# A decoder trunk on one core: VectorE takes the first convolution behind block 2's masked shares, and the third weight tile's low half behind the first normed row

## The chip, the cores and the metric

The kernel runs on one core of a Trainium2 chip. The time is what the device takes for one execution, in microseconds (us). An execution is also profiled; the profile has its own time and its own span (first instruction to last), a little shorter than that time. In the profile PE is TensorE (matmuls), PEld its weight loads, DVE is VectorE, ACT ScalarE, POOL GpSimd and SP SyncE, which issues the loads of the weights. PE, DVE and ACT each work through one list of instructions in a fixed order; an instruction whose operands are not there holds up all that stand behind it on its engine.

## The reference

The input `x` is 512 tokens of 1024 numbers. Two layers follow each other, each of three sub-layers, each with an RMS norm ahead of it that is scaled and shifted by terms made from `c`:

```python
for l in range(DEPTH):                                   # DEPTH = 2
    hn = rms_norm(h, g_ffn1[l]) * (1.0 + sc1) + sh1
    h = h + 0.5 * (1.0 + gt1) * swiglu(hn, w_ffn1_in[l], w_ffn1_out[l])     # 1024 -> 2816 -> 1024
    hn = rms_norm(h, g_mix[l]) * (1.0 + sc2) + sh2
    proj = hn @ w_mix_in[l]
    p_att, p_rwkv, p_conv = jnp.split(proj, ...)
    y_att = sliding_window_sink_attention(p_att, ...)    # window 128, blocks of 128 tokens, 2 groups of heads
    y_rwkv = rwkv7_time_mix(p_rwkv, ...)                 # a recurrence over the tokens, 4 heads of 64
    y_conv = short_conv_mix(p_conv, conv_w[l])           # three taps over time
    h = h + (1.0 + gt2) * (jnp.concatenate([y_att, y_rwkv, y_conv], axis=-1) @ w_mix_out[l])
    hn = rms_norm(h, g_ffn2[l]) * (1.0 + sc3) + sh3
    h = h + 0.5 * (1.0 + gt3) * swiglu(hn, w_ffn2_in[l], w_ffn2_out[l])
```

The convolution that the change moves is this one; `u` and the three taps are its first four operations on VectorE:

```python
b_gate, c_gate, h = jnp.split(p, [CONV_WIDTH, 2 * CONV_WIDTH], axis=-1)
u = c_gate * h
y[t] = w[2] * u[t] + w[1] * u[t - 1] + w[0] * u[t - 2]    # the convolution, written out
return b_gate * y
```

## The kernel before, in words

**Layout.** The activations stand transposed: `h` and the normed `hn` are 8 row blocks of 128 channels by 512 tokens. A matmul in full precision is three matmuls on halves of the numbers (`mm3`, lines 129 to 131): high weights by high activations, high weights by low activations, low weights by high activations. So every weight tile (128 x 1024, loaded as `wraw`) is split before use: ACT copies the high half (`wH`, line 141), DVE subtracts to get the low half (`wL`, line 143). The activations are split too: normed row `i` is `hn_t` (DVE, line 290), `hnH` (ACT, line 291), `hnL` (DVE, line 292).

**The order.** The program is written as generators and a planner in `mix` that steps them by a running clock with hand-set costs; the result is a fixed list per engine. `tc.issue_after(x)` puts what is issued inside it right behind `x` in its engine's list, `queue_behind(name)` does that with the latest instruction noted under a name, and `tc.add_manual_dep(later, earlier, ORDER)` only pins an order.

**The seam** (function `ffn`, lines 696 to 728). The last two row blocks of a feed-forward part's output, 6 and 7, are computed for the first 256 tokens, then for the second 256 (`HALVES`). While PE works on the second half, the norm of the first half is made: `stats` sums the squares over the channels (`ps_ss`, line 273), `spread` brings the result to all partitions (`ps_rstd`, line 283), `apply` makes the eight normed rows. Also in that time the next sub-layer's first three weight tiles are split by `next_weights(3)`. The next sub-layer's projector begins with those three tiles together: for each row `k` of the first half nine matmuls (three `wH` by `hnH`, then for each tile `wH` by `hnL` and `wL` by `hnH`), then the same for the second half; the fourth tile comes after. There are three such seams: from the first feed-forward part to `mix` in both layers, and from layer 1's second feed-forward part to layer 2's first.

**The convolution spot** (function `mix`, twice, once per layer). `products` (lines 827 to 975) draws 20 projected tiles from the projector and uses each; a tile lies in one of two PSUM banks of the tag `mm` until DVE or ACT has read it. For the first of the two convolutions (`q == 0`) it makes `conv_u` (line 927), its first scaling `conv_y` (line 929), two more taps (lines 930 and 931) and the gate (line 933). Between these, other generators put their work: `inverse` inverts triangular blocks for the recurrence in two levels, each `ps_x` (PE), `X` (DVE, line 1128), `ps_t` (PE), `T_` and `TT` (DVE, line 1141); the recurrence then reads `TT` in `ps_w`. `attention` goes through four blocks of 128 tokens; for each block and group the normalised shares `Sc` are transposed (`ps_pt`, PE) and masked by DVE into `pmc` (own block) and `pmp` (the block before), line 1353; `ps_av` multiplies them with `V`. The list `held` keeps the two later taps and block 2's masked shares behind the last `X` of the second level:

```python
for later in held if lev else ():
    tc.add_manual_dep(later.ins, new.ins.name, ORDER, reason="the inverse goes first")
```

Of the kernel before, what the change touches and what calls it, by code (L numbers as in the profile page):

```python
# [8 lines left out]
F32 = mybir.dt.float32  # L9
F32R = mybir.dt.float32r  # L10
I32 = mybir.dt.int32
AF = mybir.ActivationFunctionType
ALU = mybir.AluOpType
AXL = mybir.AxisListType
ORDER = mybir.DependencyInfo(mybir.DependencyClass.NoSync, mybir.DependencyReason.DATA)
SYNC = mybir.DependencyInfo(mybir.DependencyClass.Sync, mybir.DependencyReason.DATA)

P = 128
D = 1024
T = 512  # L20
L = 2
KD = D // P
# [48 lines left out]
def trunk_kernel(ctx, tc, ins, out, layers=L, phases=("ffn1", "mix", "ffn2")):  # L71
    nc = tc.nc
# [4 lines left out]
    wp = ctx.enter_context(tc.tile_pool(name="wp", bufs=3))  # L77
# [5 lines left out]
    tt, stt, ts = nc.vector.tensor_tensor, nc.vector.scalar_tensor_tensor, nc.vector.tensor_scalar  # L83
# [51 lines left out]
    def queue_behind(name):  # L135
        return tc.issue_after(latest[name].ins) if name in latest else nullcontext()
# [97 lines left out]
    def ada_until(pool, crep, l, i):  # L234
        while todo and todo[0] <= (l, i, KD - 1):
            ada_steps(pool, crep, 1)
# [115 lines left out]
    def ffn(l, w_in, w_pair, w_out, hn, im, ss, need, then, first, ready, coming):  # L352
# [6 lines left out]
        with tc.tile_pool(name="act", bufs=1) as ap_:  # L359
# [342 lines left out]
            def next_weights(n):  # L702
                for w in raws[len(nxt) : n]:
                    nxt.append(tuple(wp.tile([P, KD, P], F32R, name=x, tag=x, bufs=4) for x in ("wH", "wL")))
                    split(*nxt[-1], w, ("act", "dve"))

            ada_until(ap_, crep, *need)
            stats, spread, apply = then()
            sqs = []
            for sl in HALVES:  # L710
                for i in (6, 7):
                    pt = psmm(BANKS[1:3])[:, : T // 2]
                    for j in range(j0, j1):
                        mm3(pt, last[i, j0 + (j - j0) // n * n], (j - j0) % n, xs[j], sl, j == j0, j == j1 - 1)
                        if sl is HALVES[1]:
                            if (i, j) == (6, j0 + 5):
                                stats(HALVES[0], sqs)
                                next_weights(3)
                            elif (i, j) == (7, j0):
                                spread(HALVES[0])  # L720
                                apply(HALVES[0])
                    if i == 6:
                        residual(pt, i, cg, ss, sl)
                        if sl is HALVES[0]:
                            next_weights(1)
                    else:
                        sqs = [last_residual(pt, i, cg, ss, sl)]
# [6 lines left out]
    def mix(l, hn, ss, mp, then, ready):  # L734
# [35 lines left out]
        cm = small_.tile([P, KD], F32, name="cm", tag="cg")  # L770
        ts(cm, mod[l, 5], 1.0, None, ALU.add)

        done, held, turns = set(), [], []
        k_, r_, v_, yr = {}, {}, {}, {}
        got = {}

# [50 lines left out]
        def products():  # L827
# [93 lines left out]
            for q in range(2):  # L921
                pt = yield from tile_()
                cc = EA("conv_c")
                nc.scalar.copy(pt.like(cc), pt.view)
                pt = yield from tile_()
                u = EA("conv_u")
                tt(pt.like(u), pt.view, pt.like(cc), ALU.mult)
                cv = mp.tile([P, T], F32, name="conv_y", tag="cv", bufs=1) if q == 0 else EA("conv_y")
                ts(cv, u, cwp[:, 4 + q : 5 + q], None, ALU.mult)
                held.append(stt(cv[:, 1:], u[:, : T - 1], cwp[:, 2 + q : 3 + q], cv[:, 1:], ALU.mult, ALU.add))  # L930
                held.append(stt(cv[:, 2:], u[:, : T - 2], cwp[:, q : q + 1], cv[:, 2:], ALU.mult, ALU.add))
                pt = yield from tile_()
                tt(pt.like(cv), pt.view, pt.like(cv), ALU.mult)
                yc.append(cv)
# [361 lines left out]
        def attention():  # L1296
# [62 lines left out]
            for b in range(NB):  # L1359
                qs = slice(b * P, (b + 1) * P)  # L1360
                pm = []
                both = yield from scores(b)
                dens = [softmax(b, g, Sc) for g, Sc in enumerate(both)]
                for g, (Sc, (den, es)) in enumerate(zip(both, dens)):
                    yield 1.06 * (g == 0), 6.4 if g == 0 else 1.2
                    tt(den, den, es, ALU.add)
                    nc.vector.reciprocal(den, den)
                    share = tt(Sc, Sc, den.unsqueeze(2).to_broadcast([P, 4, P]), ALU.mult)
                    for later in turns if (b, g) == (2, 0) else ():
                        tc.add_manual_dep(later.ins, share.ins.name, ORDER, reason="shares go first")  # L1370
                    yield 0, 1.4
                    pm.append(turned(b, Sc))
                yield 0.4, 3.0
                po = psum([P, 4, P], "ps_av")
                for n in range(len(pm[0])):
                    for g in range(2):
                        t, src = pm[g][n]
                        m = pe(po[rows[g]].rearrange("p i q -> p (i q)"), V[:, src, rows[g]], t, start=n == 0, stop=n == len(pm[0]) - 1)
                        together(m, made[0])
                free[0] = nc.scalar.copy(qr[:, :, qs], po)  # L1380
                yield 1.9, 1.0
# [349 lines left out]
```

## Time and profile before

| | us |
|---|---|
| median of 3 runs | 1795.22 (1794.1 to 1796.64) |
| the profiled execution | 1792.58 |
| its span | 1790.8 |
| PE busy | 1766.0 |
| PEld busy (beside PE) | 1613.3 |
| DVE busy | 1384.6 |
| ACT busy | 856.5 |
| POOL busy | 148.3 |

The mean granted clock of PE in the profiled execution is 0.999 of full speed. PE is the engine that is nearly always busy, so the table's other rows matter only where PE waits for one of them. A row of the timeline is a run of like instructions: start, length from the first start to the last end, engine, line, operation, tiles, shapes, count; in brackets the time for which the engine had stood idle and the instruction that released it. Since matmuls overlap, the distance of their starts tells more of PE than their lengths.

### The profile page before, as it was taken

What the parts mean: (1) busy time and instruction counts of PE and PEld (TensorE: products, weight loads), DVE (VectorE), ACT (ScalarE), POOL (GpSimd) and SP (SyncE); (2) the same over time, 40 slices, a digit from 0 to 9 for tenths busy, and PEclk for the clock granted to TensorE, in tenths of its full rate; (3) what the DMA queues carried; (4) which work ended last, traced back from release to release, by engine and by line L of the source; (5) the groups of instructions that cost most, each with busy time, mean ns of one, the idle gap of its engine ahead of it and who ended that gap; (6) DMA issues with size and microseconds to landing.
All of it is one profiled execution on the core that took longest, in us unless ns stands there. A gap on an engine that the chain in (4) does not pass through costs nothing.

```text
span 1790.8 us, 34026 instructions
## 1 busy us (share of the span) xinstructions
PE 1766.0 (99%) x13952; PEld 1613.3 (90%) x13952; DVE 1384.6 (77%) x2224; ACT 856.5 (48%) x1324; POOL 148.3 (8%) x233
## 2 busy tenths in 40 slices
PE   9999999999999999999999999999999999999998
PEld 7898999987778999899899989999877798999998
DVE  7877678867768877677888776887686788864897
ACT  7452354364444554255355514543654345533563
POOL 0101001101000001100100020010000000010000
PEclk9999999999999999999999999999999999999999
DMA  9667867523133666877737687773321427684764
GB/s 378 219 185 265 227 191 214 188 76 91 42 120 100 172 192 219 265 199 202 246 96 203 175 294 199 200 228 116 112 67 39 142 80 204 183 243 133 202 172 112
DMA packets 95436, 313.08 MB, mean 175 GB/s; under 512 B 10864, under 2 KB 13168, under 8 KB 94256
## 3 DMA queue, kind: packets, MB, share of 16 engines
q1 hardware_dynamic: 65088, 203.68, 33.8%
q0 software_dynamic: 30192, 107.23, 24.2%
q8 instruction: 109, 1.79, 0.4%
q14 instruction: 47, 0.39, 0.1%
HBM read 306.93 MB, written 3.93 MB: 174 GB/s over the span
## 4 chain that ended last, share of the span: by engine, by line
PE 85%; DVE 9%; ACT 3%; issue 2%; DMA 2%; SPq 0%; DVEq 0%; ACTq 0%
PE ps_mm L129 14%; PE ps_mm L130 14%; PE ps_mm L131 14%; PE ps_d L434 7%; PE ps_d L436 7%; PE ps_d L435 7%; PE ps_f L436 3%; PE ps_f L435 3%; PE ps_f L434 3%; DVE wL L143 2%; PE ps_mm L1546 2%; PE ps_g L436 2%; PE ps_g L435 2%; PE ps_g L434 2%; ACT wH L141 1%
## 5 line engine op out<-in xcount | busy, mean ns | idle before, releaser
L141 ACT CAST wH<-wraw 128x1024 fp32r<-128x1024 f32 (+2 forms) x276 | 254.3, 928 | 441.1 <-PE ps_mm L130 188.7
L143 DVE TENSOR_TENSOR wL<-wraw,wH 128x1024 fp32r<-128x1024 f32 (+2 forms) x276 | 295.4, 1074 | 112.6 <-ACT wH L141 111.8
L129 PE MATMUL ps_mm<-actH,wH 128*128 128x512 f32 (+1 forms) x700 | 253.6, 362 | 1.0 <-DVE h L343 1.0
L130 PE MATMUL ps_mm<-actL,wH 128*128 128x512 f32 (+1 forms) x700 | 252.8, 361 | 0.0
L131 PE MATMUL ps_mm<-actH,wL 128*128 128x512 f32 (+1 forms) x700 | 252.8, 361 | 0.0
L129 PE MATMUL ps_mm<-hnH,wH 128*128 128x512 f32 (+1 forms) x712 | 248.5, 354 | 3.3 <-ACT hnH L291 3.0
L130 PE MATMUL ps_mm<-hnL,wH 128*128 128x512 f32 (+1 forms) x712 | 246.4, 348 | 0.3
L131 PE MATMUL ps_mm<-hnH,wL 128*128 128x512 f32 (+1 forms) x712 | 245.5, 346 | 0.6 <-DVE wL L143 0.6
L434 PE MATMUL ps_d<-comH,wH 128*128 128x256 f32 x864 | 238.5, 276 | 0.0
L435 PE MATMUL ps_d<-comL,wH 128*128 128x256 f32 x864 | 237.6, 275 | 0.0
L436 PE MATMUL ps_d<-comH,wL 128*128 128x256 f32 x864 | 237.6, 275 | 0.0
L143 DVE TENSOR_TENSOR wL<-sum,wH 128x1024 fp32r<-128x1024 f32 x110 | 134.6, 1225 | 80.3 <-ACT wH L141 80.2
L199 DVE SCALAR_TENSOR_TENSOR wada<-wada,crep 128x1024 f32<-128x1024 f32 x128 | 153.3, 1221 | 31.6 <-DMA wada<-in_wadaT 30.9
L141 ACT CAST wH<-sum 128x1024 fp32r<-128x1024 f32 x110 | 115.1, 1047 | 120.2 <-PE ps_f L435 39.3
L434 PEld LDWEIGHTS ps_d<-comH,wH 128*128 128x128 f32 x864 | 165.8, 192 | 1.7 <-ACT s L460 1.6
L436 PEld LDWEIGHTS ps_d<-comH,wL 128*128 128x128 f32 x864 | 165.9, 192 | 0.0
L435 PEld LDWEIGHTS ps_d<-comL,wH 128*128 128x128 f32 x864 | 165.9, 192 | 0.0
L129 PEld LDWEIGHTS ps_mm<-hnH,wH 128*128 128x128 f32 x712 | 134.2, 191 | 23.7 <-issue 7.6
L131 PEld LDWEIGHTS ps_mm<-hnH,wL 128*128 128x128 f32 x712 | 136.0, 191 | 13.9 <-DVE wL L143 1.0
L130 PEld LDWEIGHTS ps_mm<-hnL,wH 128*128 128x128 f32 x712 | 136.1, 191 | 13.4 <-DVE hnL L292 1.3
L129 PEld LDWEIGHTS ps_mm<-actH,wH 128*128 128x128 f32 x700 | 132.7, 190 | 17.2 <-DVE h L343 1.9
L131 PEld LDWEIGHTS ps_mm<-actH,wL 128*128 128x128 f32 x700 | 132.7, 190 | 15.5
(426 smaller groups left out, 4005.0 us busy)
## 6 DMA issues: line engine op xcount, KB each, us to landing
wada<-in_wadaT POOLq DMA_DIRECT2D x126, 512.0 KB, 4.7
wraw<-in_wmi SPq DMA_DIRECT2D x40, 512.0 KB, 3.5
wraw<-in_w2p SPq DMA_DIRECT2D x36, 512.0 KB, 4.1
wraw<-in_w1p SPq DMA_DIRECT2D x32, 512.0 KB, 4.2
wraw<-in_w1o SPq DMA_DIRECT2D x32, 384.0 KB, 4.9
wraw<-in_w2o SPq DMA_DIRECT2D x32, 384.0 KB, 4.2
wraw<-in_w1o SPq DMA_DIRECT2D x32, 320.0 KB, 3.7
sum<-in_w2p SPq DMA_DIRECT2D x18, 512.0 KB, 4.4
```

Of the source, the lines that this page charges most:

```text
L129: mm(acc, wH, xH, start=start, stop=False)
L130: mm(acc, wH, xL, start=False, stop=False)
L131: latest["large"] = mm(acc, wL, xH, start=False, stop=stop)
L141: latest["cast"] = nc.scalar.copy(hi, src)
L143: return nc.vector.tensor_sub(lo, src, hi.bitcast(F32))
L199: stt(w, w, 1.0, crep, ALU.mult, ALU.mult, accum_out=out_)
L434: mm(acc, wH, xH, start=start and i + k == 0, stop=False, skip_group_check=True)
L435: mm(acc, wH, xL, start=False, stop=False, skip_group_check=True)
L436: mm(acc, wL, xH, start=False, stop=k == 3, skip_group_check=True)
L1546: latest["large"] = pin("PE", mm(paired(pts[n]), w, x, start=first, stop=last, skip_group_check=True))
```

## The change

Two orders are changed; no operation is added or taken away, on any engine.

At the seam, `next_weights(2)` splits only two tiles, and the new `third_weights` treats the third in two calls: the first queues its high half on ACT where it stood; the second, after the first normed row, queues its low half on DVE behind that row's `hnL`. Only then are rows 1 to 7 normed.

At the convolution spot all four operations of the first convolution (`conv_u` and the three taps) are pinned behind the last masked share of block 2; before, the last two of them were pinned behind the inverse's last `X`, and the first two were free. The second convolution's taps are no longer pinned.

```diff
+            def third_weights(parts):
+                if not parts:
+                    parts.extend(wp.tile([P, KD, P], F32R, name=x, tag=x, bufs=4) for x in ("wH", "wL"))
+                    with queue_behind("act"):
+                        nc.scalar.copy(parts[0], raws[2])
+                else:
+                    with queue_behind("norm_dve"):
+                        nc.vector.tensor_sub(parts[1], raws[2], parts[0].bitcast(F32))
+                    nxt.append(tuple(parts))
...
-            sqs = []
+            sqs, late = [], []
             for sl in HALVES:
...
                             if (i, j) == (6, j0 + 5):
                                 stats(HALVES[0], sqs)
-                                next_weights(3)
+                                next_weights(2)
+                                third_weights(late)
                             elif (i, j) == (7, j0):
                                 spread(HALVES[0])
-                                apply(HALVES[0])
+                                apply(HALVES[0], range(1))
+                                third_weights(late)
+                                apply(HALVES[0], range(1, KD))
...
                 u = EA("conv_u")
-                tt(pt.like(u), pt.view, pt.like(cc), ALU.mult)
+                taps = [tt(pt.like(u), pt.view, pt.like(cc), ALU.mult)]
                 cv = mp.tile([P, T], F32, name="conv_y", tag="cv", bufs=1) if q == 0 else EA("conv_y")
-                ts(cv, u, cwp[:, 4 + q : 5 + q], None, ALU.mult)
-                held.append(stt(cv[:, 1:], u[:, : T - 1], cwp[:, 2 + q : 3 + q], cv[:, 1:], ALU.mult, ALU.add))
-                held.append(stt(cv[:, 2:], u[:, : T - 2], cwp[:, q : q + 1], cv[:, 2:], ALU.mult, ALU.add))
+                taps.append(ts(cv, u, cwp[:, 4 + q : 5 + q], None, ALU.mult))
+                taps.append(stt(cv[:, 1:], u[:, : T - 1], cwp[:, 2 + q : 3 + q], cv[:, 1:], ALU.mult, ALU.add))
+                taps.append(stt(cv[:, 2:], u[:, : T - 2], cwp[:, q : q + 1], cv[:, 2:], ALU.mult, ALU.add))
+                if not q:
+                    first_taps.extend(taps)
...
                     pm.append(turned(b, Sc))
+                    for later in first_taps if (b, g) == (2, 1) else ():
+                        tc.add_manual_dep(later.ins, made[0].ins.name, ORDER, reason="shares go before the taps")
```

What that does to the lists is seen at three places. Lines are those of the kernel listed: 1128, 1141 and 1353 of before are 1143, 1156 and 1368 after; 927, 929, 930, 931 and 933 are 940, 942, 943, 944 and 948.

**First listing: DVE at the first seam.** `wL_3563`, `wL_3567` and `wL_3856` are the low halves of the next projector's second, third and fourth tile, `h6` is output row 6 of the second half, `hn_t_3593` (after the change `hn_t_3592`) and `hnL_3445` belong to the first normed row. Before:

```order
L143 TENSOR_TENSOR wL_3563<-wraw_3440,wH_3562 128x1024
L143 TENSOR_TENSOR wL_3567<-wraw_3442,wH_3566 128x1024
L343 SCALAR_TENSOR_TENSOR h6_91<-ps_mm_3535,cg_1443,h6_91 128x256
L143 TENSOR_TENSOR wL_3856<-wraw_3854,wH_3855 128x1024
L250 TENSOR_TENSOR ss_578<-ss_578,sq_3583 128x256
L290 SCALAR_TENSOR_TENSOR hn_t_3593<-h0_85,gmod_3460,ps_rstd_3590 128x256
L290 SCALAR_TENSOR_TENSOR hn_t_3597<-h0_85,gmod_3460,ps_rstd_3590 128x256
L290 SCALAR_TENSOR_TENSOR hn_t_3601<-h2_87,gmod_3460,ps_rstd_3590 128x256
L292 SCALAR_TENSOR_TENSOR hnL_3445<-hn_t_3593,mod0_3_1450,hnH_3444 128x256
```

After:

```order
L143 TENSOR_TENSOR wL_3563<-wraw_3440,wH_3562 128x1024
L343 SCALAR_TENSOR_TENSOR h6_91<-ps_mm_3535,cg_1443,h6_91 128x256
L290 SCALAR_TENSOR_TENSOR hn_t_3592<-h0_85,gmod_3460,ps_rstd_3589 128x256
L250 TENSOR_TENSOR ss_578<-ss_578,sq_3582 128x256
L290 SCALAR_TENSOR_TENSOR hn_t_3597<-h0_85,gmod_3460,ps_rstd_3589 128x256
L292 SCALAR_TENSOR_TENSOR hnL_3445<-hn_t_3592,mod0_3_1450,hnH_3444 128x256
L714 TENSOR_TENSOR wL_3567<-wraw_3442,wH_3566 128x1024
L292 SCALAR_TENSOR_TENSOR hnL_3447<-hn_t_3597,mod0_3_1450,hnH_3446 128x256
L290 SCALAR_TENSOR_TENSOR hn_t_3601<-h2_87,gmod_3460,ps_rstd_3589 128x256
```

The third tile's `wL` has moved behind the first row's `hnL`; the fourth tile's `wL_3856` has left the piece: it stands behind the eighth row's `hnL`, ahead of the second half's statistics.

**Second listing: DVE at the convolution spot of layer 1.** `X1` and `X0` are the second level's, `pmc` and `pmp` block 2's masked shares, `ps_mm_4955` the projected tile that `conv_u` reads, `wL_5373` and `wL_5726` low halves of later weight tiles. Before:

```order
L927 TENSOR_TENSOR conv_u_5099<-ps_mm_4955,conv_c_4947 128x512
L929 TENSOR_SCALAR conv_y_5101<-conv_u_5099,par_93 128x512
L143 TENSOR_TENSOR wL_5373<-wraw_5371,wH_5372 128x1024
L1128 TENSOR_TENSOR X1_4715<-ps_x_5133,con_83 64x256
...
L930 SCALAR_TENSOR_TENSOR conv_y_5101<-conv_u_5099,par_93,conv_y_5101 128x511
L1353 TENSOR_TENSOR pmc_5126<-ps_pt_5121,con_83 128x512
L931 SCALAR_TENSOR_TENSOR conv_y_5101<-conv_u_5099,par_93,conv_y_5101 128x510
L1353 TENSOR_TENSOR pmp_5128<-ps_pt_5121,con_83 128x512
L1353 TENSOR_TENSOR pmc_5189<-ps_pt_5184,con_83 128x512
L1353 TENSOR_TENSOR pmp_5191<-ps_pt_5184,con_83 128x512
L1141 TENSOR_TENSOR TT0_4519<-TT0_4519,ps_t_5199 128x256
...
L1141 TENSOR_TENSOR TT1_4520<-TT1_4520,ps_t_5201 128x256
L1141 TENSOR_TENSOR TT1_4520<-TT1_4520,ps_t_5202 64x256 x2
L143 TENSOR_TENSOR wL_5726<-wraw_5724,wH_5725 128x768
```

After, from the first share on (`wL_5373` and the six `X` stand ahead of it):

```order
L1368 TENSOR_TENSOR pmc_5126<-ps_pt_5121,con_83 128x512
L1368 TENSOR_TENSOR pmp_5128<-ps_pt_5121,con_83 128x512
L1368 TENSOR_TENSOR pmc_5189<-ps_pt_5184,con_83 128x512
L1368 TENSOR_TENSOR pmp_5191<-ps_pt_5184,con_83 128x512
L940 TENSOR_TENSOR conv_u_5099<-ps_mm_4955,conv_c_4947 128x512
L143 TENSOR_TENSOR wL_5726<-wraw_5724,wH_5725 128x768
L942 TENSOR_SCALAR conv_y_5101<-conv_u_5099,par_93 128x512
L1156 TENSOR_TENSOR TT0_4519<-TT0_4519,ps_t_5199 128x256
L943 SCALAR_TENSOR_TENSOR conv_y_5101<-conv_u_5099,par_93,conv_y_5101 128x511
...
L1156 TENSOR_TENSOR TT1_4520<-TT1_4520,ps_t_5201 128x256
L1156 TENSOR_TENSOR TT1_4520<-TT1_4520,ps_t_5202 64x256 x2
```

The shares follow the `X` at once, `conv_u` and its taps stand behind them and among the `TT`, and the 128x768 `wL` has moved from behind the last `TT1` to ahead of the first `TT0`.

**Third listing: PE at the same spot**, with the waits that an instruction carries (`DVE_49` is the count of finished DVE instructions). `ps_mm_5245` is a later tile of the projector, in the bank that `ps_mm_4955` had. Before:

```order
L791 MATMUL ps_t_5201<-TT1_4520,X1_4715 64x64 x2
L129 MATMUL ps_mm_5245<-hnH_3444,wH_5106 128x512
L130 MATMUL ps_mm_5245<-hnL_3445,wH_5106 128x512
L131 MATMUL ps_mm_5245<-hnH_3444,wL_5107 128x512
L791 MATMUL ps_av_5249<-pmc_5126,V_4028 64x512 [waits DVE_49]
L791 MATMUL ps_av_5249<-pmc_5189,V_4028 64x512 [waits DVE_49]
L791 MATMUL ps_av_5249<-pmp_5128,V_4028 64x512
L791 MATMUL ps_av_5249<-pmp_5191,V_4028 64x512 [waits DVE_49]
```

After:

```order
L804 MATMUL ps_t_5201<-TT1_4520,X1_4715 64x64 x2
L129 MATMUL ps_mm_5245<-hnH_3444,wH_5106 128x512 [waits DVE_49]
L130 MATMUL ps_mm_5245<-hnL_3445,wH_5106 128x512
L131 MATMUL ps_mm_5245<-hnH_3444,wL_5107 128x512
L804 MATMUL ps_av_5249<-pmc_5126,V_4028 64x512
L804 MATMUL ps_av_5249<-pmc_5189,V_4028 64x512
L804 MATMUL ps_av_5249<-pmp_5128,V_4028 64x512
L804 MATMUL ps_av_5249<-pmp_5191,V_4028 64x512
```

The four `ps_av` have lost their waits on DVE, and the first matmul of `ps_mm_5245` ahead of them has got one.

More of the change, by code (lines that the diff above doesn't have):

```diff
@@ L771, in mix @@
         ts(cm, mod[l, 5], 1.0, None, ALU.add)
-        done, held, turns = set(), [], []
+        done, held, turns, first_taps = set(), [], [], []
         k_, r_, v_, yr = {}, {}, {}, {}
```

## The prediction

> **What bounds the kernel now.** I read the page's busy shares first, then the waits of TensorE (PE), then the timeline at the places where those waits fall.
>
> ```profile
> PE 1766.0 (99%) x13952; PEld 1613.3 (90%) x13952; DVE 1384.6 (77%) x2224; ACT 856.5 (48%) x1324; POOL 148.3 (8%) x233
> ```
>
> PE is busy for 1766.0 of the span's 1790.8 us, and the change removes no matmul. All that an order can win is the 24.8 us in which PE stands, and what the clock does to its busy time. The waits of PE say who ends these stands (columns: total us, times, longest):
>
> ```profile
> PE ps_mm L129 <- ACT hnH L291: 3.0, 5, 0.7
> PE ps_ss L273 <- DVE ss L250: 2.4, 4, 0.7
> PE ps_t L791 <- DVE X L1128: 2.2, 2, 1.1
> PE ps_av L791 <- DVE pmp L1353: 1.1, 2, 0.5
> ```
>
> These four rows, 8.7 us together, are the two places of the change: the first two belong to the seam where one projector follows a feed-forward part (three times in the program), the last two to the spot in `mix` where the first convolution meets block 2's shares (once per layer, so twice). VectorE (DVE) is named in three of them and stands behind the fourth, since `hnH` on ScalarE (ACT) is made from DVE's `hn_t`. At both places DVE has a queue of ready work and PE waits for an item that is not at its head.
>
> The first seam, all engines, in order of time (start, length; in brackets the idle time ahead and who ended it):
>
> ```profile
> 345.05 2.93 ACT L141 CAST wH<-wraw 128x1024 fp32r<-128x1024 f32 x3
> 346.12 2.36 DVE L143 TENSOR_TENSOR wL<-wraw,wH 128x1024 fp32r<-128x1024 f32 x2 [0.77 <-ACT wH L141]
> 346.41 0.38 PE L283 MATMUL ps_rstd<-con,rstd 128*128 128x128 f32 x2
> 348.40 0.48 DVE L343 SCALAR_TENSOR_TENSOR h<-ps_mm,cg,h 128x256 f32<-128x256 f32 x1
> 348.79 1.22 DVE L143 TENSOR_TENSOR wL<-wraw,wH 128x1024 fp32r<-128x1024 f32 x1
> 348.97 0.42 ACT L254 ACTIVATE sq<-h 128x256 f32<-128x256 f32 x1 [0.99 <-DVE h L343]
> 349.53 0.28 PE L131 MATMUL ps_mm<-actH,wL 128*128 128x256 f32 x1
> 349.92 0.42 DVE L250 TENSOR_TENSOR ss<-ss,sq 128x256 f32<-128x256 f32 x1
> 350.26 1.26 DVE L290 SCALAR_TENSOR_TENSOR hn_t<-h,gmod,ps_rstd 128x256 f32<-128x256 f32 x3
> 350.40 0.38 PE L273 MATMUL ps_ss<-ones_r,ss 128*128 128x1 f32 x2 [0.59 <-DVE ss L250]
> 350.77 1.31 ACT L291 ACTIVATE hnH<-hn_t,mod 128x256 fp32r<-128x256 f32 x3 [1.39 <-DVE hn_t L290]
> 351.33 0.60 PE L129 MATMUL ps_mm<-hnH,wH 128*128 128x256 f32 x3 [0.55 <-ACT hnH L291]
> 351.43 0.48 DVE L292 SCALAR_TENSOR_TENSOR hnL<-hn_t,mod,hnH 128x256 fp32r<-128x256 f32 x1
> 351.83 0.48 DVE L290 SCALAR_TENSOR_TENSOR hn_t<-h,gmod,ps_rstd 128x256 f32<-128x256 f32 x1
> 351.97 0.38 PE L130 MATMUL ps_mm<-hnL,wH 128*128 128x256 f32 x1
> ```
>
> Before PE can go on it needs `ss` and the first normed row, and both stand behind three subtractions `wL` of 1.14 us each (346.12 twice, 348.79 once: second, third and fourth tile). The last old matmul issues at 349.53, and these issue every 0.11 us, so `ps_ss` could start at 349.64; it starts at 350.40, 0.76 late. Two of these and the next is due at 350.62: `hnH` is read at 351.33, 0.71 late. Three tiles read it, so `hnL` is due at 351.67 and read at 351.97, 0.30 late. One seam costs PE about **1.7 us** (1.77 by these starts, of which I count 1.67, since changing from one matmul shape to another costs some 0.1 anyway).
>
> **The seam after the change.** DVE's operations are the same; their order is that of the first listing. By row durations (starts 0.39 apart for 128x256, as 351.43 to 351.83; 1.14 for 128x1024): the second tile's `wL` at 346.12, `h` at 347.25, `hn_t` of row 0 at 347.65 (its `ps_rstd` came at 346.41). `sq` follows on ACT at 348.0, when `h` and the casts of 345.05 are done, so `ss` runs 348.48 to 348.90, the second `hn_t` from 348.80, `hnL` of row 0 until 349.68, and the third tile's `wL` 349.60 to 350.82. PE wants `ss` at 349.64 and the first `hnH` at 349.86: both are there, and 0.76 and 0.71 go. `hnL` of row 0 is wanted at 350.19: there. The third `wL` is wanted by the ninth matmul of row 0, at about 350.83: just there.
>
> What is late next is the rows behind it. `hnL` of row 1 ends at about 351.2, wanted at 351.27: with the hand-over to PE I put 0.2. `hnL` of row 2 ends at 352.8, wanted at 352.5: 0.3. From row 3 (353.6) DVE's two operations per row, 0.79 us, are quicker than PE's nine matmuls, 1.0. The second half's `ps_rstd` now follows a row earlier (only nine matmuls, 1.0 us, cover `hn_t` 0.48, `hnH` 0.50 and three hand-overs): another 0.3 to 0.4. The fourth tile's `wL` moves behind row 7, to about 356.2, and delays nothing before the fourth tile, which is two halves of 72 matmuls away. So 0.6 to 1.0 us remain; the gain is 0.65 to 1.07 per seam. I take 0.9, three times: **−2.7 us**. ACT keeps its order, and on SP one small load passes one weight load that is needed tiles later: nothing.
>
> **The convolution spot**, first PE, then DVE:
>
> ```profile
> 483.28 0.38 PE L131 MATMUL ps_mm<-hnH,wL 128*128 128x512 f32 x1
> 484.75 1.16 PE L791 MATMUL ps_t<-TT,X 64*64 64x64 f32 x64 [1.09 <-DVE X L1128]
> 487.30 1.24 PE L791 MATMUL ps_av<-pmc,V 128*64 128x512 f32 x3 [0.54 <-DVE pmp L1353]
> 489.76 0.48 PE L129 MATMUL ps_mm<-hnH,wH 128*128 128x512 f32 x1
> 492.31 0.89 PE L791 MATMUL ps_w<-AX,TT 64*64 64x128 f32 x24
> ```
>
> ```profile
> 479.63 0.68 DVE L927 TENSOR_TENSOR conv_u<-ps_mm,conv_c 128x512 f32<-128x512 f32 x1
> 480.75 1.22 DVE L143 TENSOR_TENSOR wL<-wraw,wH 128x1024 fp32r<-128x1024 f32 x1
> 482.00 2.60 DVE L1128 TENSOR_TENSOR X<-ps_x,con 64x256 f32<-64x256 f32 x6
> 484.64 0.75 DVE L930 SCALAR_TENSOR_TENSOR conv_y<-conv_u,par,conv_y 128x511 f32<-128x511 f32 x1
> 487.16 0.68 DVE L1353 TENSOR_TENSOR pmc<-ps_pt,con 128x512 f32<-128x512 f32 x1
> 487.76 0.68 DVE L1353 TENSOR_TENSOR pmp<-ps_pt,con 128x512 f32<-128x512 f32 x1
> 491.56 0.96 DVE L143 TENSOR_TENSOR wL<-wraw,wH 128x768 fp32r<-128x768 f32 x1
> ```
>
> PE stands 1.25 us ahead of `ps_t` (483.50 to 484.75), some 0.6 ahead of `ps_av`, and `ps_av` itself takes 2.46 (487.30 to 489.76) where an undisturbed one takes 1.87, from its first pass to the work behind it:
>
> ```profile
> 461.94 1.08 PE L791 MATMUL ps_av<-pmc,V 128*64 128x512 f32 x4
> 463.81 1.16 PE L791 MATMUL ps_xv<-vN,K 64*64 64x64 f32 x64
> ```
>
> Together 2.4 us per layer that seem there for the taking. After the change `conv_u` and the scaling behind it (479.63 to 480.75, 1.12 us) no longer stand ahead of `X`: it ends at 483.49, and `ps_t` starts at 483.63, 1.12 earlier. The shares follow at once and end at 485.98.
>
> But the third listing shows a **new wait**. PE's next projector matmul, `ps_mm_5245`, waits for DVE: its accumulator takes the bank of `ps_mm_4955`, the tile that `conv_u` reads, and `conv_u` now stands behind four shares. With starts 0.60 apart (487.16 to 487.76) it begins at 485.89 and ends at 486.57. PE, done with `ps_t` at 484.72, stands until about 486.64: 1.92 us, and all of PE's later work is queued behind. Then three matmuls, the `ps_av` at 487.49 without waits, and the next projector matmul at 489.36, 0.40 ahead of 489.76, so that `ps_w` would be reached at 491.91 instead of 492.31.
>
> There the rest goes. `ps_w` reads `TT1`, the last of DVE's chain. DVE works without a gap from 479.63 to here, so the same operations end at the same time, except that the 128x768 `wL`, 0.93 us, now stands ahead of the `TT`s instead of behind: `TT1`, done at 491.53 before, is done at about 492.4. PE waits 0.5 us for it. Net per layer +0.1 (0 to +0.2), **+0.2 us** for both. At this spot DVE is the bound, and the edit only chooses where PE stands.
>
> **The clock.** Windows of 3.41 us on one grid (columns: length, busy us and instructions of PE, PEld, DVE, ACT, POOL, granted PE clock, DMA share, GB/s):
>
> ```profile
> 349.02:352.43 3.41, 2.23 (x17) 1.76 (x16) 3.41 (x8) 1.76 (x5) 0.99 (x2) 1.00 0.37 109
> 352.43:355.85 3.42, 3.42 (x19) 3.42 (x18) 3.42 (x10) 1.95 (x4) 0.00 (x0) 0.50 0.24 85
> 1232.99:1236.41 3.42, 2.28 (x19) 2.00 (x18) 3.42 (x8) 1.15 (x3) 0.98 (x2) 1.00 0.14 17
> 1236.41:1239.82 3.41, 3.26 (x25) 2.94 (x26) 3.41 (x10) 2.11 (x5) 0.00 (x0) 1.00 0.45 175
> 482.13:485.54 3.41, 2.31 (x62) 1.84 (x63) 3.31 (x8) 0.83 (x1) 0.00 (x0) 1.00 0.32 115
> 485.54:488.96 3.42, 2.88 (x37) 1.51 (x27) 3.41 (x7) 0.00 (x0) 0.00 (x0) 1.00 0.02 5
> ```
>
> At the first seam a window with PE busy for 2.23 us was followed by one at clock 0.50, in which half of 3.42, 1.7 us, is lost. Windows with 2.28 and 2.31 were followed by full clock. So the line lies near 2.25 here, and whether a stand of this size falls into one window is chance: one seam of three was hit, so I count 1 hit × 1.7 = 1.7 us per execution before. After, the seams' stands are short and apart: none. But the convolution's 1.92 us in one piece leaves at most 1.5 busy of a window that holds all of it, which it does for (3.41 − 1.92) / 3.41 = 44% of positions; a hit costs 1.7 less the 0.5 that PE would wait at `ps_w`: 2 × 0.44 × 1.2 = 1.05. Net **−0.7 us** (−1.7 to +0.7, by none or both hit).
>
> The Trainium skill ("TensorE: Matmul & The Clock Gate", "HAM oscillation — how this bites in real kernels") gives as the rule "no PE-idle gaps >~3.4µs". By that rule no stand here would touch the clock, and the sum would be −2.5 instead of −3.2; the 0.50 behind a window with 1.2 us of idle time speaks against it.
>
> **The sum**: −2.7 + 0.2 − 0.7 = −3.2 us. The profiled execution took 1792.58 (span 1790.8), 2.64 under the median of 1795.22; it gives 1789.4 for an execution like it, and **1792.0** against the median. What a measurement can tell from no change is about 0.2%, 3.6 us: the forecast lies just inside, and whether it shows as faster is nearly even.
>
> **Rivals.**
>
> *The convolution's stands go too* (1787.2, chance 0.15). If the bank or `TT1` does not hold PE, 2.4 us per layer come on top: 1792.0 − 4.8 = 1787.2. For it: the two rows of waits, 3.3 us. Against: the wait that the listing shows, and DVE's chain without a gap.
>
> *The edits win next to nothing* (1794.2, chance 0.18). DVE's order at the seam only passes the stand on: if rows 1 and 2 and the second half each wait for the full hand-over, the gain is 0.65 per seam, −1.95; with +0.2 and both convolution spots hit, +0.7, that is −1.05. For it: DVE is busy in the whole of both seam windows (3.41 and 3.42), so its work is not shorter by anything.
>
> *Slower: the clock falls at both convolution spots* (1796.8, chance 0.11). If the line is met in two windows at each spot, since the slow window is itself followed by the wait at `ps_w`, four windows cost 4 × 1.7 = 6.8, less 1.0 of slack and the 1.7 of the seam's hit now: +4.1, and with −2.7 and +0.2 the sum is +1.6; with the seams' lower bound, −1.95, it is +2.4, and with a seam hit left standing +4.1. It decides from PE busy under 2.25 in a window. For it: 1.92 us in one piece is more than any stand now. Against: the one hit in this trace lasted a single window.
>
> **Chances.** Forecast 0.56 (own range 1790.0 to 1793.8; 0.27 of it beyond 0.2%), first rival 0.15 (all but 0.01 beyond it), second 0.18 (all within), slower 0.11 (0.08 beyond). Faster 0.41, same 0.51, slower 0.08. The range goes down to 1788.0, half-way into the first rival with its bounds, and up to 1796.5, leaving out most of the slower case.
>
> **What would show it.** Right: at the three seams the waits for `ss` and the first `hnH` are gone, a small wait for `hnL` in their place; the wait for `X` shrinks to about 0.1; a new wait of PE on `conv_u` of 1.9, twice, and one of 0.5 on `TT`. Wrong: a wait of 0.3 or more on the third tile's `wL` at a seam (my margin there is 0.01); no wait on `conv_u`; `ps_w` starting more than 1 us before 492.31 less the seam's gain; or a clock of 0.50 behind either convolution spot.

## The result, and the profile after

| | before | after |
|---|---|---|
| median, us | 1794.01 (22 runs, 1791.19 to 1797.2) | 1790.4 (22 runs, 1789.03 to 1793.5) |
| ratio | | 0.9981, 95% interval 0.9975 to 0.9987 |
| profiled execution, its span | 1792.58, 1790.8 | 1789.03, 1787.3 |
| PE busy | 1766.0 | 1764.7 |

The change makes the kernel faster by 0.19%, 3.4 us (2.3 to 4.5). A second measurement, beside other runs of before, gave 0.9984 (0.9975 to 0.9993). The forecast was 3.2 us (1792.0 against the 1795.22 known then), just inside the 0.2% that it took as no change; the result lies there too.

The waits of PE in the profile after (total us, times, longest), those of the two places and the ones that answer to them:

```profile
PE ps_mm L129 <- DVE conv_u L940: 3.7, 2, 1.9
PE ps_mm L129 <- ACT hnH L291: 1.1, 3, 0.7
PE ps_w L804 <- DVE TT L1156: 0.8, 2, 0.4
PE ps_ss L273 <- DVE ss L250: 0.5, 1, 0.5
PE ps_mm L130 <- DVE hnL L292: 0.2, 1, 0.2
```

The waits for the sums of squares have gone from 2.4 us to 0.5 and those for `hnH` from 3.0 to 1.1; what is left of both is mostly at the passages from `mix` to the second feed-forward part, which the change does not touch. The waits for the last `X` (2.2) and for the shares (1.1) are gone, and 3.7 + 0.8 us for `conv_u` and `TT` have come: more than they were.

The same seam as in the prediction, after the change, in order of time:

```profile
345.74 1.23 DVE L143 TENSOR_TENSOR wL<-wraw,wH 128x1024 fp32r<-128x1024 f32 x1 [0.77 <-ACT wH L141]
346.88 0.48 DVE L343 SCALAR_TENSOR_TENSOR h<-ps_mm,cg,h 128x256 f32<-128x256 f32 x1
347.28 0.48 DVE L290 SCALAR_TENSOR_TENSOR hn_t<-h,gmod,ps_rstd 128x256 f32<-128x256 f32 x1
347.96 0.42 DVE L250 TENSOR_TENSOR ss<-ss,sq 128x256 f32<-128x256 f32 x1 [0.20 <-ACT sq L254]
348.69 0.48 DVE L292 SCALAR_TENSOR_TENSOR hnL<-hn_t,mod,hnH 128x256 fp32r<-128x256 f32 x1
349.09 1.22 DVE L714 TENSOR_TENSOR wL<-wraw,wH 128x1024 fp32r<-128x1024 f32 x1
349.15 0.28 PE L131 MATMUL ps_mm<-actH,wL 128*128 128x256 f32 x1
349.26 0.28 PE L273 MATMUL ps_ss<-ones_r,ss 128*128 128x1 f32 x2
349.40 0.36 PE L129 MATMUL ps_mm<-hnH,wH 128*128 128x256 f32 x1
350.38 0.36 PE L131 MATMUL ps_mm<-hnH,wL 128*128 128x256 f32 x1
350.76 0.38 PE L130 MATMUL ps_mm<-hnL,wH 128*128 128x256 f32 x1
```

`ps_ss` follows the last old matmul after 0.11 us (0.87 before), the first normed row after another 0.14 (0.93 before). The third tile's `wL` ends at 350.31 and the first matmul that reads it starts at 350.38: in time, with 0.07 us to spare.

The convolution spot after the change, PE and then DVE:

```profile
480.72 1.16 PE L804 MATMUL ps_t<-TT,X 64*64 64x64 f32 x64
483.74 0.48 PE L129 MATMUL ps_mm<-hnH,wH 128*128 128x512 f32 x1 [1.86 <-DVE conv_u L940]
484.58 1.08 PE L804 MATMUL ps_av<-pmc,V 128*64 128x512 f32 x4
486.45 0.48 PE L129 MATMUL ps_mm<-hnH,wH 128*128 128x512 f32 x1
489.45 1.98 PE L804 MATMUL ps_w<-AX,TT 64*64 64x128 f32 x64 [0.38 <-DVE TT L1156]
```

```profile
482.40 0.68 DVE L1368 TENSOR_TENSOR pmp<-ps_pt,con 128x512 f32<-128x512 f32 x1
483.00 0.68 DVE L940 TENSOR_TENSOR conv_u<-ps_mm,conv_c 128x512 f32<-128x512 f32 x1
488.12 1.28 DVE L1156 TENSOR_TENSOR TT<-TT,ps_t 128x256 f32<-128x256 f32 x3
```

All four steps of the prediction at this spot are there: `ps_t` without a wait, a stand of 1.86 us for `conv_u`, `ps_av` without a wait, and a stand of 0.38 for the last `TT`.

**Where the time went.** The traces have the same PE instructions, so the start of one and the same matmul in both shows how far after is ahead (us; minus is earlier):

| what PE has just passed | ahead there | the step |
|---|---|---|
| the opening | −0.38 | −0.38 |
| first seam (fourth tile done) | −2.91 | −2.53 |
| first convolution spot (`ps_w`) | −2.86 | +0.05 |
| `ps_o`, layer 1 | −2.80 | +0.06 |
| from `mix` to the feed-forward part, layer 1 | −2.39 | +0.42 |
| second seam | −3.44 | −1.01 |
| 1091 us, a wait of 0.17 for ACT | −3.27 | +0.17 |
| third seam | −4.26 | −0.99 |
| second convolution spot | −4.19 | +0.03 |
| `ps_o`, layer 2 | −3.52 | +0.67 |
| the end | −3.54 | |

Each seam gives 1.0 us of stands, the first another 1.5 because no slow stretch of the clock follows it. The convolution spot gives nothing. The remaining steps, and 0.04 us just ahead of the second seam that the table's last column leaves out, belong to no edited place: the +0.42 follows a fall of the clock at 570.69 us, and the wait ahead of `ps_o`, for which the profile names no releaser, varies with the execution: 1.17 and 0.90 us before, 1.23 and 1.57 in this profile, 1.24 and 1.20 in the second one of the same kernel.

### The profile page after: what moved, and what is told of

The parts are those of the page before. It is cut to its first block, busy times and chain, and to the rows that moved or that the text cites. A ratio compares the mean times of both kernels' runs of the same rounds, so it can differ in the third digit from the quotient of the medians.

```text
span 1787.3 us, 34022 instructions
## 1 busy us (share of the span) xinstructions
PE 1764.7 (99%) x13952; PEld 1612.4 (90%) x13952; DVE 1385.0 (77%) x2224; ACT 856.0 (48%) x1324; POOL 148.9 (8%) x233
## 4 chain that ended last, share of the span: by engine, by line
PE 83%; DVE 8%; ACT 3%; DMA 2%; issue 2%; POOL 0%; DVEq 0%; ACTq 0%; SPq 0%; POOLq 0%
PE ps_mm L129 13%; PE ps_mm L130 13%; PE ps_mm L131 13%; PE ps_d L434 7%; PE ps_d L435 7%; PE ps_d L436 7%; PE ps_f L436 3%; PE ps_f L435 3%; PE ps_f L434 3%; PE ps_mm L1563 2%; PE ps_g L434 2%; PE ps_g L435 2%; PE ps_g L436 2%; DVE wL L143 2%; DMA third<-in_w1p 1%
## 5 line engine op out<-in xcount | busy, mean ns | idle before, releaser
L143 DVE TENSOR_TENSOR wL<-wraw,wH 128x1024 fp32r<-128x1024 f32 (+2 forms) x273 | 291.4, 1071 | 105.5 <-ACT wH L141 104.5
```

Of the source, the lines that this page charges most:

```text
L143: return nc.vector.tensor_sub(lo, src, hi.bitcast(F32))
```

## The experiments

Theory A is that of the prediction: the seams carry the gain, and at the convolution spot DVE's chain to the last `TT` sets when the recurrence can start, so PE only stands elsewhere. A measurement is given as the ratio of the time to that of before (with its 95% interval) and, behind it, the difference in us.

### Each edit alone

The first kernel is the change without its second part, the second is the kernel before with that part alone:

```diff
 # seam alone: of the convolution, before's lines
-                taps = [tt(pt.like(u), pt.view, pt.like(cc), ALU.mult)]
+                tt(pt.like(u), pt.view, pt.like(cc), ALU.mult)
...
-                    for later in first_taps if (b, g) == (2, 1) else ():
```

> The seam's edit alone; the convolution's orders are those of before. Theory A (the three seams carry the whole gain, the convolution spot gives back what it takes): the same time as with both edits, 3.4 to 3.6 us under before, ratio 0.998; the waits for the last X (2 x 1.1) and for the masked shares (2 x 0.5) stay, those for the sums of squares and the first normed row at the three seams are gone. Theory B (both edits give): about half of it, 1.5 to 2 us, ratio 0.999.

> The convolution's edit alone; the seams are those of before. Theory A: no change, 0 to +0.3 us (ratio 1.000); TensorE waits 1.9 us for conv_u and 0.4 for the last TT in each layer, and the recurrence's first product starts within 0.2 us of where it starts before. Theory B: 1.5 to 2 us faster (ratio 0.999). If a stand of 1.9 us in one piece makes the clock fall, about 1 us slower on average, and the trace shows a stretch at 0.50 behind it.

Measured: the seam alone 0.9973 (0.9963 to 0.9984), 4.8 us faster; the convolution alone 1.0004 (0.9996 to 1.0013). Theory B, that both give, falls. In the trace of the seam alone the three seams give 2.54, 1.00 and 1.01, as in the change, and the convolution spots 0.00. In the trace of the convolution alone its two spots cost 0.05 and 0.04, with these waits:

```profile
PE ps_mm L129 <- DVE conv_u L927: 3.7, 2, 1.9
PE ps_w L791 <- DVE TT L1143: 0.8, 2, 0.4
```

The seam alone looks faster than both edits (0.9973 against 0.9981 and 0.9984), but the intervals overlap. The places differ by only 0.05 us per layer; the clock differs by more, as the table of granted clocks further down shows.

### Is the wait for the bank the loss, or DVE's chain?

The convolution's edit with `conv_u` let go:

```diff
                 if not q:
-                    first_taps.extend(taps)
+                    first_taps.extend(taps[1:])
```

> As the convolution's edit alone, but conv_u is not pinned, only the scaling and the two taps are; so the bank that the next projector tile needs is free early. Theory A (the last TT on VectorE sets where the recurrence's first product starts): the 1.9 us wait for conv_u is gone in both layers, X ends 0.4 us earlier than before instead of 1.1, the wait moves to the recurrence's first product, and since the 768-wide subtraction stays behind the last TT here, at most 0.7 us per layer is won: 0 to -1.3 us in all. Theory C (the wait for the bank is itself the loss): 3.7 us faster than with conv_u pinned, ratio 0.998 to before.

Measured: 0.9992 (0.9983 to 1.0), 1.4 us faster. The waits:

```profile
PE ps_w L791 <- DVE TT L1143: 2.1, 2, 1.1
PE ps_t L791 <- DVE X L1130: 1.1, 2, 0.6
```

The wait for `conv_u` is gone, 3.7 us of it, and `ps_w` starts only 0.59 and 0.60 us earlier: PE now stands 1.1 us there. So the bank was not the loss (theory C would be 3.7 us). What little is won against the convolution's edit alone is the 768-wide subtraction, which the scheduler leaves behind the last `TT` in this kernel.

### Shortening DVE's chain

`conv_u` free, and the rest of the convolution behind the last `TT` (in `invert`) and no longer behind the shares:

```diff
+                        if lev and q != qs[0]:
+                            for later in first_taps:
+                                tc.add_manual_dep(later.ins, new.ins.name, ORDER, reason="the inverse goes before the taps")
```

> conv_u is not pinned; the scaling, the two taps and with them the gate stand behind the last TT of the inverse instead of ahead of it (and the two later taps are no longer behind the last X). Theory A: VectorE's chain to the last TT is 2 us shorter, so TensorE does not wait at the recurrence's first product; what is won ahead of it (0.4 at the last X, some 0.8 at the masked shares) stays: 1.1 to 1.25 us per layer, 2.3 in all, ratio 0.9987. Theory D (TensorE's gain here is lost to a later wait on VectorE, at block 3's shares): within 0.5 us of before.

Measured: 0.9985 (0.9977 to 0.9994), 2.7 us faster. The total is near theory A's, the places are not. `ps_w` starts 1.73 us earlier in the first layer and 1.74 in the second, more than the 1.25 expected, and 1.0 us of that is lost at the next wait, as theory D has it for a place further on:

```profile
492.51 0.69 DVE L935 TENSOR_TENSOR conv_y<-ps_mm,conv_y 128x512 f32<-128x512 f32 x1
493.11 0.76 DVE L1324 COPY_PREDICATED Sc<-con,ps_sc 128x256 f32<-128x256 int32 x2
493.93 1.13 PE L791 MATMUL ps_sc<-kt,qr 64*128 64x256 f32 x8 [0.95 <-DVE Sc L1324]
```

The copies of block 3's scores stand behind the four convolution operations, and PE's next scores wait for them. So DVE's chain is the bound here from the last `X` on, and the place where PE feels it depends on what stands last in it.

### An order that keeps the gain

The seam's edit, and the convolution's operations shared out: `conv_u` is free, nothing is pinned behind the shares, the scaling and the first later tap stand behind the last `TT`, the second later tap and the gate behind the first score copies of block 3, where DVE even then idles for 2.47 us:

```diff
+                            for later in first_taps[:2]:
+                                tc.add_manual_dep(later.ins, new.ins.name, ORDER, reason="the inverse goes before the taps")
...
                     if i0 == 0:
+                        for later in first_taps[2:] if b == 3 else ():
+                            tc.add_manual_dep(later.ins, free[0].ins.name, ORDER, reason="the scores go before the taps")
```

> The seam's edit, and at the convolution another order: conv_u free, the scaling and the first later tap behind the last TT, the second later tap and the gate behind block 3's first score copies. Theory A: beside the seam's gain, 1.7 us per layer are won ahead of the recurrence's first product, as with the taps behind the last TT, and the wait of 0.95 us for block 3's scores that followed there is gone, since the scores' copies no longer stand behind four convolution operations: 3.4 us under the seam's edit alone, some 1786 us, ratio 0.9955. Theory D (the gain here is taken back at the next wait on VectorE, wherever that is): within 1 us of the seam's edit alone, ratio 0.997.

Measured: 1785.41 us, 0.9952 (0.994 to 0.9964), 8.6 us faster than before and the fastest kernel of this study. The convolution spots give 1.72 and 1.73 us, and nothing is taken back behind them:

```profile
488.50 0.75 DVE L943 SCALAR_TENSOR_TENSOR conv_y<-conv_u,par,conv_y 128x511 f32<-128x511 f32 x1
489.17 0.77 DVE L1337 COPY_PREDICATED Sc<-con,ps_sc 128x256 f32<-128x256 int32 x2
489.83 0.75 DVE L944 SCALAR_TENSOR_TENSOR conv_y<-conv_u,par,conv_y 128x510 f32<-128x510 f32 x1
493.77 0.78 DVE L1337 COPY_PREDICATED Sc<-con,ps_sc 128x256 f32<-128x256 int32 x2 [2.47 <-ACT Sc L1336]
```

### Which tile's move counts at the seam

The change moves two subtractions: the third tile's on purpose, the fourth's along with it. Here the third stays where it was and the fourth alone is pinned behind the eighth normed row:

```diff
-            ws.extend(load_w(s, behind=places.get(len(ws))) for s in srcs[len(ws) : n])
+            for s in srcs[len(ws) : n]:
+                ws.append(load_w(s, behind=places.get(len(ws))))
+                if "half" in latest:
+                    tc.add_manual_dep(latest["w"].ins, latest.pop("half").ins.name, ORDER, reason="the rows go first")
...
                                 apply(HALVES[0])
+                                if nxt:
+                                    latest["half"] = latest["norm_dve"]
```

> The seam by its other half: the third tile's low half stays where it is before, and only the fourth tile's is pinned behind the eighth normed row; the convolution is that of before. Theory A (what made TensorE wait at the seam is how much work VectorE does ahead of the first row, whichever tile it belongs to): the first normed row is there in time, the sums come 0.25 us late, the first low row 0.3 late; 1.0 to 1.15 us per seam are won, so it is as fast as the seam's edit alone or up to 0.5 us faster, ratio 0.997 to 0.998. Theory E (the third tile's move is what counts): at most half of the seam's gain, ratio 0.999 or above.

Measured: 0.997 (0.9959 to 0.9982), 5.4 us faster. The second and third seam give 1.07 and 1.16 us (1.01 and 0.99 with the change). DVE at its first seam:

```profile
345.94 2.36 DVE L143 TENSOR_TENSOR wL<-wraw,wH 128x1024 fp32r<-128x1024 f32 x2 [0.77 <-ACT wH L141]
348.61 0.47 DVE L290 SCALAR_TENSOR_TENSOR hn_t<-h,gmod,ps_rstd 128x256 f32<-128x256 f32 x1
349.24 0.42 DVE L250 TENSOR_TENSOR ss<-ss,sq 128x256 f32<-128x256 f32 x1 [0.15 <-ACT sq L254]
```

So theory E falls: the edit's words name the third tile, but the fourth tile's 1.14 us out of the way of the first row are enough, and moving the third too adds nothing that can be seen. Whether the third tile's move without the fourth's would do as much was not run.

The same with the other convolution order:

> The other half of the seam (only the fourth tile's low half moved) with the other order at the convolution. Theory A: as with the seam's edit in its place, or up to 0.5 us faster, ratio 0.995 to 0.9955. Theory E: 2 us slower than that.

Measured: 0.9961 (0.9949 to 0.9973), 1786.47 us. That overlaps the other combination (0.9952) and, by the times alone, theory E's 2 us as well. The places decide: 1.07 and 1.15 us at the second and third seam, 1.72 and 1.73 at the convolution spots, each as large as there or larger; the 0.8 us by which its profile is longer come from the opening (+0.45) and from waits at no edited place.

### A long stand at the convolution, and the clock

This is the kernel with the taps behind the last `TT`, but with `conv_u` there too. PE's list also changes here: the recurrence's first product moves ahead of the projector's matmul.

```diff
-                    first_taps.extend(taps[1:])
+                    first_taps.extend(taps)
```

> conv_u and all that follows it stand behind the last TT, so that TensorE stands for some 3.4 us in one piece ahead of the recurrence's first product, in each layer; the seams are those of before. Stands alone: some 4 us per layer where it is 2.4 before, 3 us slower in all, ratio 1.0017. If the clock falls when TensorE stands for most of a window of 3.41 us, a stretch at 0.50 follows each stand, up to 1.7 us each on top, ratio 1.0035, and the trace shows it; if it does not fall at this spot whatever the length, the clock stays 1.00 there.

Measured: 1.0041 (1.0029 to 1.0054), 7.4 us slower. The windows from the stand on (columns as in the prediction):

```profile
485.64:489.05 3.41, 0.48 (x17) 0.51 (x21) 3.34 (x8) 0.00 (x0) 0.00 (x0) 1.00 0.24 69
489.05:492.46 3.41, 3.06 (x29) 1.84 (x23) 3.28 (x6) 1.78 (x3) 0.00 (x0) 0.50 0.12 46
492.46:495.88 3.42, 3.42 (x9) 0.65 (x6) 0.77 (x2) 0.07 (x1) 0.00 (x0) 0.50 0.00 0
1376.52:1379.93 3.41, 0.04 (x3) 0.00 (x0) 3.35 (x8) 0.00 (x0) 0.00 (x0) 1.00 0.16 32
1379.93:1383.34 3.41, 3.37 (x35) 2.45 (x35) 3.26 (x7) 1.25 (x3) 0.00 (x0) 0.50 0.24 91
```

Both stands of 3.42 us are followed by a fall, the first for two windows. That is the mechanism of the prediction's slower rival. In this trace the two spots lose 5.1 and 3.3 us against before, of which the stands explain some 1.0 each (3.42 us, less the 2.4 us of waits that were there before), so at this length the falls cost more than the stands.

### Filling the seam's stand

Six matmuls whose result nobody reads are put where PE stands at each seam, in the kernel before:

```diff
+            if nxt:
+                pf = psum([P, T // 2], "ps_fill")
+                for j in range(6):
+                    mm(paired(pf), last[7, j0][0][:, 0], weave(xs[j0][0][:, HALVES[1]]), start=j == 0, stop=j == 5)
             stats(HALVES[1], sqs)
```

> The kernel before with six matmuls of 256 columns added at each seam, between the last matmul of the feed-forward part and the sums of squares; nobody reads their result, so the outputs are the reference's. They need 0.66 us of TensorE where it stands for 0.76, so no stand grows by more than 0.1 us. Theory F (the clock falls behind a window of 3.41 us in which few columns are streamed, under some 3350): the seams' windows rise from 3200 columns to over 4500, the profile shows no stretch at 0.50 behind any of the three seams, and the time falls by up to 1.7 us, ratio 0.9991 to 1.0. Theory G (the stand itself, or the number of idle stretches, makes it fall): a stretch at 0.50 behind one of the seams as in the traces so far, ratio 1.000.

> The change as it is, once more, beside the same runs of before as the filled seam. Theory A: 3.4 to 4.8 us under before, ratio 0.9973 to 0.9981, that is between its first measurement and that of the seam's edit alone.

Measured: the filled seam 0.9996 (0.9988 to 1.0005); the change beside it 0.9984 (0.9975 to 0.9993). The filler stands where PE stood, and no slow stretch follows any of the three seams:

```profile
350.58 0.83 PE L731 MATMUL ps_fill<-actH,wH 128*128 128x256 f32 x6
351.47 0.38 PE L273 MATMUL ps_ss<-ones_r,ss 128*128 128x1 f32 x2
352.26 0.60 PE L129 MATMUL ps_mm<-hnH,wH 128*128 128x256 f32 x3 [0.41 <-ACT hnH L291]
```

The mean granted clock of each execution says more than one profile can. A window of 3.41 us at 0.50 takes 3.41 × 0.5 / 1790, about 0.001, from it, and in all twelve profiled executions its third decimal gives the number of their windows at 0.50 (0.998 for the two with the taps behind the last `TT`, 0.995 for the five of the long stand; the fall behind the last matmul, at the program's end, takes at most 0.0005 in these profiles and is not counted). So the executions that were not profiled can be counted too:

| kernel | executions | with clock 1.000 | mean number of windows at 0.50 |
|---|---|---|---|
| before (beside the experiments) | 63 | 20 | 1.05 |
| the change | 33 | 3 | 1.24 |
| the convolution's edit alone | 11 | 2 | 1.36 |
| the four kernels with either seam order and no stand for `conv_u` | 24 | 17 | 0.29 |
| before with filled seams | 11 | 9 | 0.18 |

So the stands at the seams are what let the clock fall there: with them filled, or with either seam order, most executions have no fall. Each fall is also seen in the time: in the first 31 of these executions of before, the 12 with none, the 11 with one and the 7 with two took 1792.26, 1793.75 and 1795.07 us on average, 1.4 us more for each. The filled kernel's time holds both that gain and no change in its interval. What the clock counts stays open: the filler adds columns and shortens the stand at once, so theory F and theory G are not told apart, and the 3350 columns of theory F are an estimate that no run here tests.

The change's second profile shows what the first did not, a fall at the convolution spot:

```profile
480.47:483.89 3.42, 1.56 (x67) 1.23 (x66) 3.39 (x7) 0.83 (x1) 0.00 (x0) 1.00 0.03 5
483.89:487.30 3.41, 3.41 (x9) 1.32 (x11) 3.35 (x7) 0.00 (x0) 0.00 (x0) 0.50 0.35 115
```

Past that spot the lead over before is 1.24 us smaller than ahead of it, where the first profile lost 0.05.

## Why the prediction was right

**The seam's stands.** Right, and its size nearly: 1.0 us at each seam, where the prediction took 0.9 from a range of 0.65 to 1.07. The two large waits are gone, the third tile's `wL` is just in time, and the small waits left (at the third seam 0.21 and 0.15 us for `hnL` and 0.22 for `hnH`, at the first 0.11 for `hnH`) are those that it named. The step it did not take apart is which of the two moved subtractions matters; the fourth tile's alone is enough. One reading was too generous: of the 5.4 us of its first two rows, 2.0 belong to the passages from `mix` to the second feed-forward part (0.67 us at 571.12, 0.66 at 575.51 and at 1459.30), not to the three seams. The sum does not use that total; it goes by the timeline of the first seam.

**The convolution spot.** Right in all its terms: 1.86 us for `conv_u` (1.92 forecast), 0.38 for `TT` (0.5), `ps_t` 1.12 us earlier (1.12), and +0.05 and +0.03 net per layer (0 to +0.2). The kernel with `conv_u` free shows that the reason was right too: without the wait for the bank PE waits for `TT` instead. The first rival, in which these stands go, had 2.4 us per layer; the best order reached 1.7, by shortening what stands ahead of `TT`, which this change does not do.

**The clock.** This is the term that the runs do not bear out, and the total does not show it. Its two parts are of the right kind. The five profiles with the old, unfilled seam have a fall behind one seam each, the one per execution that was assumed, and the eighteen seams of the six profiles with either new order have none; the fall at the first seam cost 1.5 us, not 1.7. The convolution's stand was followed by a fall in one of six profiled cases, where 44% was assumed, and that one cost 1.24 us against 1.2. But the granted clocks of all executions put the net near nothing instead of −0.7 us: the change has 1.24 windows at 0.50 per execution, before has 1.05. The kernels without the new stand have 0.29, so the seams lose some 0.8 falls and the rest of the change brings some 0.95 back. By the prices above that is −1.1 and +1.2 us, an estimate. Where the falls of the executions without a profile lie is not recorded; of the two in profiles of the change one lies behind the convolution's stand, one at 570.69 us, on the way from `mix` to the feed-forward part. The prediction also named a clock of 0.50 behind either convolution spot as a sign that it was wrong, although its own sum counts on 0.88 of them per execution; the second profile has one.

The line at 2.25 us of PE busy, which was to tell which windows are followed by a fall, does not hold either:

```profile
481.94:485.35 3.41, 1.61 (x7) 0.83 (x9) 3.41 (x7) 0.00 (x0) 0.00 (x0) 1.00 0.02 5
485.35:488.77 3.42, 3.42 (x20) 1.89 (x16) 3.33 (x7) 0.59 (x1) 0.00 (x0) 1.00 0.38 115
567.27:570.69 3.42, 2.90 (x26) 2.71 (x25) 2.53 (x5) 0.71 (x2) 0.00 (x0) 1.00 0.57 153
570.69:574.10 3.41, 3.16 (x16) 3.07 (x15) 2.05 (x6) 1.53 (x3) 0.00 (x0) 0.50 0.53 154
```

In the first profile of the change a window with 1.61 us busy, which holds all but 0.06 us of the convolution's stand, was followed by full clock, and one with 2.90 by half. PE busy in a window does not tell.

**The sum.** −2.7, +0.2 and −0.7 were forecast. The trace has −3.0 for the stands at the seams, +0.08 at the convolution, and −1.5 + 0.42 for the falls of the clock; the opening and the waits at no edited place, −0.38, +0.17 and +0.73, make up the rest of the 3.5 us between the two spans. That is one pair of executions, in which the change's only fall cost little. Over all executions the clock gives about nothing, which leaves the −2.9 us of the stands beside the 3.4 us (2.3 to 4.5) measured. So it is in part luck that the total came within 0.2 us of the forecast: the seams gave 0.3 us more than forecast and the clock about 0.7 less. The sum without the clock, −2.5, would lie in the interval too, so the total does not test that term.

**The rivals.** *The convolution's stands go too* fell with the convolution alone, 1.0004. *The edits win next to nothing* fell: the seams' gain is at the upper end of its range. *The clock falls at both convolution spots* did not come true in either profile of the change; a single fall there did, and the long stand shows its price. Two falls in one execution are not rare, though: 11 of the 33 executions of the change have the clock for it, at places that are not recorded.

## What to carry to other kernels

When a wait goes, follow the engine that was waited for to the next thing that it owes: at the convolution the change removed 2.4 us of waits per layer and won none of it, because VectorE's list up to `TT` had not become shorter. An order pays when it moves work past the last item that is waited for, into idle time of that engine, as the order that kept 1.7 us per layer does. Look at what else an edit moves: here a subtraction that the edit does not name was enough for the whole of the seam's gain. And count the clock's falls over all executions, not in one or two profiles: the change took them away at the seams and brought about as many back.

## What the runs showed of the hardware

A stand of PE far shorter than a window of 3.41 us can halve the clock for the next window: behind the seams' two stands of 0.59 and 0.55 us it did so at one of the three seams in each of five profiles, behind the 1.86 us at the convolution in one of six cases, behind 3.42 us in two of two. With the seams' stands filled 9 of 11 executions kept the full clock, against 5 of 21 of before beside them. Three more falls, at 570.69, 571.92 and 577.79 us in the profiles of the change, of the taps behind the last `TT` and of the long stand, lie on the way from `mix` to the feed-forward part, where no experiment was made. The Trainium skill ("TensorE: Matmul & The Clock Gate", "HAM oscillation — how this bites in real kernels") names idle gaps of more than about 3.4 µs; the long stands agree, and the short ones show that a gap below it is not safe. What is counted stays open, since neither the length of the stand nor PE's busy time orders these cases.
